# Other costs in the engine model by which a two-tile transformer kernel orders its instructions

## The chip, the cores and the metric

One Trainium2 chip, one core of it. The metric is the device time of one execution in microseconds (us); a run's time is given as the median of several executions. PE is TensorE, DVE is VectorE, ACT is ScalarE, POOL is GpSimd and SP is SyncE, whose queue issues the DMA transfers.

## What is computed

Two blocks of a transformer, one after the other, on x of 256 tokens by 1024 features, in float32, with a memory of 256 tokens. Cut to its outline:

```python
x = first_block(x, mem, ...)      # h = rms_norm(x); p = h @ w_in  (q, k, v, z, xbc, dt, gates)
#   merged = sigmoid(ga) * (stick_breaking_attention(q, k, v) @ w_br_att)
#          + sigmoid(gs) * (ssd_branch(z, xbc, dt) @ w_br_ssm)
#   x += rms_norm(merged @ w_mix_out)
#   x += rms_norm(memory_cross_attention(rms_norm(x), rms_norm(mem)) @ w_xo)
#   x += rms_norm((silu(gate) * up) @ w_down)          # gate, up = rms_norm(x) @ w_gu
x = second_block(x, mem_2, ...)   # two layers: fox (gated causal attention), then mla (latent attention, rope)
#   x += concat(mixer(h), memory_cross(h)) @ w_out
#   u = conv3(rms_norm(x) @ w_up);  x += (silu(u_gate) * u_val) @ w_dn
```

## The kernel before

The 256 tokens are two tiles of 128. A float32 product is made of three products of parts: each value is split into a high part in float32r and a low part, the rest; a product adds high times high, high times low and low times high in PSUM. Weights come by DMA in units of [128, 1024] (512 KB) into one of four raw buffers (`wr`), are copied to a high part (`wh`, normally on ScalarE) and subtracted to a low part (`wl`, on VectorE or GpSimd), and up to ten split units are held. Each unit is used by both tiles and then freed.

The program is written as threads (Python generators): `main(0)` and `main(1)` for the tiles, and others for attention lanes, the state space model, the memory's keys and the preparing of weights. A thread yields what it wants next: an instruction for VectorE, ScalarE or GpSimd (line 263 on), a buffer, a bank of PSUM, or "may TensorE go on" (`start`, lines 351 to 394). `run` (line 396) goes on, over and over, with the thread whose want can start earliest by a model of the engines; small weights for priorities and turns (`BASE`, `TUNE`, lines 56 to 64) are added to that time. What it picks is emitted at once, so this choice fixes the order of instructions in every engine's queue. Each queue then runs in that order on the chip, and waits where an operand isn't ready.

The model (`Model`, line 181) holds one time for each engine, and for every stretch of a buffer the times of its last write and read. `regs` (line 236) puts an instruction at the later of its engine's time and of its operands' times, and adds its cost; `after` (line 210) adds a latency of 0.17 us where another engine wrote the operand, and `SAME` (0.1) where the same one did. The costs are formulas of the number n of elements in a partition, in `Engine` (lines 268 to 292), and numbers given with each product (`mm`, line 538):

```python
if eng == "ACT":   c = 0.00083 * n + 0.08 + 0.09 * small + (0.15 if len(outs) > 1 else 0)
elif eng == "DVE": c = (0.00052 if one and not psum else 0.00104) * n + 0.07 + 0.05 * (small > 0)
else:              c = 0.0021 * n + 0.1          # GpSimd; a power: 0.165 * n + 0.3
```

Some instructions have two forms, of which `start` takes the one that would end first after a bias: a copy on ScalarE or VectorE (`copy`, line 552), the low part of a weight on VectorE or GpSimd (`prepare_low`, line 493: `E.tensor_tensor(L, raw, H, subtract) for E in (V, G)`, GpSimd put back by `POOL`, 0.8 us, or 0.4 in the stage `ssd`).

The whole program is run twice (`model_kernel`, lines 2051 to 2054): a first pass that emits nothing and finds in which order the weight units are wanted, and a second one that emits the instructions and splits the units in that order. The model serves both.

Lines of the profile: 539 is the matmul in `mm`, 543 the transpose in `tr`, 547 a DMA, and 290 the call of any VectorE, ScalarE or GpSimd instruction (the helper in `Engine`).

Of the kernel before, what the change touches and what calls it, by code (L numbers as in the profile page):

```python
# [46 lines left out]
# row table of short vectors  # L47
# [18 lines left out]
NB = 10      # split weight units held  # L66
RAW = 4      # raw weight units held
# [28 lines left out]
class Arena:  # L96
    """Places buffers in one SBUF tile: in the smallest gap, the large ones at its end."""
# [38 lines left out]
class Split:  # L136
    """A value as two float32r parts whose sum is the float32 value."""
# [11 lines left out]
class Joint:  # L149
    """The splits of both tiles' [128 features, 8, 128 tokens]"""  # L150
# [13 lines left out]
class Spare:  # L164
    """A split unit's place that is lent for something else"""
# [15 lines left out]
class Model:  # L181
    """Rough times of the engines, by which the order of instructions is chosen."""

    LAT = 0.17

    def __init__(self):
        self.t = {"PE": 0.0, "DVE": 0.0, "ACT": 0.0, "POOL": 0.0, "DMA": 0.0}
        self.index = {e: i for i, e in enumerate(self.t)}
        self.s = {}
# [14 lines left out]
    def state(self, t):  # L204
        if t not in self.s:
            # times of the last write and the last read, and the engines of these
            self.s[t] = np.zeros((4, ARENA // 8 + 1))
        return self.s[t]

    def after(self, regs, eng, rows):  # L210
        e = 0.0
        for t, lo, hi in regs:
            a = self.state(t)
            for i in rows:
                x = a[2 * i, lo:hi]
                j = x.argmax()
                x = x[j] + ((SAME if eng and not i else 0.0) if a[2 * i + 1, lo + j] == eng else self.LAT)
# [4 lines left out]
    def ready(self, ap, rows=(0,)):  # L222
        """When the tensor engine can use it"""
# [4 lines left out]

    def deps(self, eng, outs, ins):
        i = self.index[eng]  # L230
        # two engines don't read a bank at once
# [17 lines left out]
class Op:  # L249
    """An instruction to be put into its engine's queue in its turn."""  # L250

    def __init__(self, eng, emit, cost, outs, ins, func=None):
        self.eng, self.emit, self.cost, self.func = eng, emit, cost, func
# [4 lines left out]
class Engine:  # L258
    """Makes the instructions of an engine, with their rough costs."""
# [4 lines left out]
    def __getattr__(self, op):  # L264
# [3 lines left out]
        def call(*a, **k):  # L268
# [6 lines left out]
            psum = any(x.tensor.name.startswith("pa") for x in [out] + ins)  # L275
            small = sum(size(x) == 1 for x in ins)
            if eng == "ACT":
# [1856 lines left out]
```

## Time and profile before

| | |
|---|---|
| time of a run, median of 3 | 1334.74 us (1333.91 to 1334.86) |
| span of the profiled execution | 1330.6 us, 22067 instructions; its own time was not recorded apart |
| mean granted TensorE clock | 0.993 of 2.4 GHz |
| matmul busy (PE), weight load busy (PEld) | 97%, 86% of the span |
| VectorE, ScalarE, GpSimd busy | 68%, 61%, 21% |
| HBM | 217.95 MB moved by DMA, 163 GB/s over the span |
| chain that ended last, by engine | PE 79%, DVE 9%, POOL 5%, ACT 3%, issue 2%, DMA 2% |

A matmul's record runs from its issue to its modelled end and overlaps the next one's, so records are longer than the distance from one to the next, and a busy PE can hide short gaps. The span leaves out what lies before the first and after the last instruction, some 4 us here (1334.7 less 1330.6). Idle time of an engine is listed with what ended it.

### The profile page before, as it was taken

The numbers are of one execution on the slowest core, as the hardware profiler recorded it, in microseconds if no ns is written. First come the engines' busy times: TensorE is split into PE (matmuls) and PEld (weight loads), VectorE is DVE, ScalarE is ACT, GpSimd is POOL, SyncE is SP. The second block draws the span as 40 slices with busy tenths as digits, with TensorE's granted clock in tenths as the row PEclk, the third lists the DMA queues.
The fourth block names the chain that finished last, engine by engine and source line by source line (L and its number), as shares of the span: only waits on it lengthen the run. The fifth ranks groups of instructions, "written<-read, shape, count | busy, mean of one in ns | idle before, by whom it ended". The sixth has DMA issues, their size and how long they took to land.

```text
span 1330.6 us, 22067 instructions
## 1 busy us (share of the span) xinstructions
PE 1289.8 (97%) x8376; PEld 1146.3 (86%) x8376; DVE 909.7 (68%) x1471; ACT 816.8 (61%) x1481; POOL 285.1 (21%) x364
## 2 busy tenths in 40 slices
PE   8999999999999999999998899998999989999998
PEld 6989998898888887999997788788999867799997
DVE  6567688877677537655556567898665897786664
ACT  6567677766646547544456566785554785865552
POOL 3052203333022002000014521102111463031110
PEclk9999999999999999999999999998999999999999
DMA  8632543544664624756552343566654333365650
GB/s 270 219 112 96 195 154 107 180 158 143 216 211 159 227 73 143 246 183 188 190 192 96 127 143 112 191 221 221 190 185 144 115 112 99 131 223 189 185 173 32
DMA packets 62457, 217.95 MB, mean 164 GB/s; under 512 B 7440, under 2 KB 7568, under 8 KB 62352
## 3 DMA queue, kind: packets, MB, share of 16 engines
q1 hardware_dynamic: 62352, 216.56, 49.9%
q8 instruction: 65, 1.06, 0.3%
q14 instruction: 40, 0.33, 0.1%
HBM read 215.48 MB, written 1.05 MB: 163 GB/s over the span
## 4 chain that ended last, share of the span: by engine, by line
PE 79%; DVE 9%; POOL 5%; ACT 3%; issue 2%; DMA 2%; SPq 0%; DVEq 0%; POOLq 0%; ACTq 0%
PE pa L539 75%; DVE arena L290 6%; POOL arena L290 4%; PE pa L543 3%; DVE wl L290 2%; ACT arena L290 2%; POOL small L290 1%; ACT wh L290 1%; DVE arena_r L290 1%; DMA wr<-in_w_in 1%; ACT arena_r L290 0%; DMA arena<-in_mem 0%; DMA wr<-in_w_up 0%; DMA wr<-in_w_dn 0%; SPq L547 0%
## 5 line engine op out<-in xcount | busy, mean ns | idle before, releaser
L539 PE MATMUL pa<-wh,arena_r 128*128 128x512 f32 (+2 forms) x1812 | 590.8, 395 | 3.6 <-DVE arena_r L290 1.6
L290 DVE TENSOR_TENSOR wl<-wr,wh 128x1024 fp32r<-128x1024 f32 (+2 forms) x353 | 432.4, 1233 | 219.9 <-ACT wh L290 214.4
L290 ACT ACTIVATE wh<-wr 128x1024 fp32r<-128x1024 f32 (+3 forms) x393 | 406.2, 1044 | 246.5 <-PE pa L539 200.2
L539 PE MATMUL pa<-arena_r,wh 128*128 128x256 f32 (+2 forms) x2736 | 495.5, 283 | 0.0
L539 PEld LDWEIGHTS pa<-arena_r,wh 128*128 128x128 f32 (+2 forms) x2736 | 425.6, 190 | 4.3 <-issue 0.3
L539 PEld LDWEIGHTS pa<-wh,arena_r 128*128 128x128 f32 x1812 | 342.3, 190 | 73.2 <-DVE arena_r L290 3.3
L539 PE MATMUL pa<-arena_r,wl 128*128 128x256 f32 (+2 forms) x1368 | 385.5, 282 | 0.0
L539 PE MATMUL pa<-wl,arena_r 128*128 128x512 f32 (+2 forms) x906 | 353.2, 390 | 4.2 <-DVE wl L290 4.1
L539 PEld LDWEIGHTS pa<-arena_r,wl 128*128 128x128 f32 (+2 forms) x1368 | 259.9, 190 | 0.2
L290 POOL TENSOR_TENSOR wl<-wr,wh 128x1024 fp32r<-128x1024 f32 (+2 forms) x53 | 131.0, 2476 | 568.0 <-ACT wh L290 543.7
L539 PEld LDWEIGHTS pa<-wl,arena_r 128*128 128x128 f32 x906 | 172.0, 190 | 35.4 <-DVE wl L290 5.4
L290 ACT ACTIVATE arena<-pa 128x512 f32<-128x512 f32 (+4 forms) x142 | 78.5, 563 | 73.8 <-PE pa L539 58.9
L290 DVE SCALAR_TENSOR_TENSOR arena<-pa,cols,arena 128x255 f32<-128x255 f32 (+2 forms) x208 | 89.1, 476 | 31.2 <-ACT arena L290 29.6
L290 DVE TENSOR_TENSOR arena<-arena 128x512 f32<-128x512 f32 (+4 forms) x117 | 90.8, 792 | 23.1 <-POOL arena L290 13.3
L290 ACT ACTIVATE arena<-arena 128x512 f32<-128x512 f32 (+5 forms) x126 | 76.6, 615 | 33.7 <-DVE arena L290 30.6
L539 PE MATMUL pa<-arena 128*64 128x128 f32 (+4 forms) x888 | 91.2, 286 | 3.2 <-POOL arena L290 1.7
L539 PEld LDWEIGHTS pa<-arena 128*64 128x64 f32 (+3 forms) x888 | 78.1, 160 | 16.4 <-issue 5.5
L543 PE MATMUL pa<-ident,arena 128*128 128x128 f32 (+3 forms) x494 | 73.1, 278 | 18.1 <-DVE arena L290 14.0
L543 PEld LDWEIGHTS pa<-ident,arena 128*128 128x128 f32 (+3 forms) x494 | 56.8, 138 | 33.9 <-DVE arena L290 19.1
L290 POOL TENSOR_SCALAR small<-small 128x1 f32<-128x1 f32 x38 | 17.4, 459 | 265.6 <-ACT arena L290 186.9
L290 ACT ACTIVATE arena<-pa,cols 128x256 f32<-128x256 f32 x92 | 44.8, 566 | 28.2 <-PE pa L539 28.2
L290 ACT ACTIVATE arena<-pa,small 128x128 f32<-128x128 f32 (+4 forms) x126 | 44.5, 416 | 21.9 <-PE pa L539 21.6
(123 smaller groups left out, 769.8 us busy)
## 6 DMA issues: line engine op xcount, KB each, us to landing
wr<-in_w_up SPq DMA_DIRECT2D x96, 512.0 KB, 4.0
wr<-in_w_in SPq DMA_DIRECT2D x80, 512.0 KB, 4.3
wr<-in_w_gu SPq DMA_DIRECT2D x44, 512.0 KB, 4.1
wr<-in_w_dn SPq DMA_DIRECT2D x44, 512.0 KB, 4.2
wr<-in_w_down SPq DMA_DIRECT2D x22, 512.0 KB, 4.0
wr<-in_w_fox SPq DMA_DIRECT2D x20, 512.0 KB, 3.3
wr<-in_w_br_ssm SPq DMA_DIRECT2D x16, 512.0 KB, 4.2
wr<-in_w_xkv SPq DMA_DIRECT2D x16, 512.0 KB, 4.1
```

The source lines that it names most:

```text
L290: emit = (lambda: f(*a, **k)) if f else (lambda: None)
L539: self.T.matmul(out, l, r, start=start, stop=stop, skip_group_check=True)
L543: self.T.transpose(out, in_, self.const["ident"][:k, :k])
```

## The change

Comments and docstrings are left out of the changed file, which changes no instruction. The rest lies in the model; no thread asks for another instruction, and `BASE`, `TUNE` and the other weights keep their values.

- **Latencies.** Instead of 0.17 us for any other engine: by the writer (`LAT`: PE 0.205, DVE 0.118, ACT 0.136, POOL 0.06) plus by the reader (`USE`: PE 0.02, POOL 0.05, DMA 0.1); for the same engine `OWN` (DVE 0.118, ACT 0.136, POOL 0.03) instead of `SAME`.
- **Products.** `mm` no longer takes a cost; `product` works it out from the shape and type. A product of 256 columns in float32r goes from 0.109 to 0.120 us, of 512 from 0.216 to 0.227, a pair's half in float32 from 0.2 to 0.115.
- **A shared port.** One time, `port`, for the VectorE instructions with two operands in SBUF, or with one and none in PSUM, and for GpSimd's with any input: such an instruction starts no earlier than the last of them ended, in `start` as in `regs`.
- **The matmul clock.** After a wait of TensorE over a limit, its instructions cost 1.9 times as much for 3 us.
- **Costs.** GpSimd's instructions cost more: 0.25 us plus 0.0023 n (a power 0.45 plus 0.165 n), copies and memsets less than that; ScalarE's differ by 0.03 us at most, but for those with an accumulated sum; a DMA lands 0.4 us later.

```diff
-    LAT = 0.17
+    LAT = {"PE": 0.205, "DVE": 0.118, "ACT": 0.136, "POOL": 0.06, "DMA": 0.0}
+    USE = {"PE": 0.02, "DVE": 0.0, "ACT": 0.0, "POOL": 0.05, "DMA": 0.1}
+    OWN = {"PE": 0.0, "DVE": 0.118, "ACT": 0.136, "POOL": 0.03, "DMA": 0.0}
...
-                x = x[j] + ((SAME if eng and not i else 0.0) if a[2 * i + 1, lo + j] == eng else self.LAT)
+                k = int(a[2 * i + 1, lo + j])
+                x = x[j] + ((0.0 if i else self.own[eng]) if k == eng else self.lat[k] + self.use[eng])
...
+    def product(l, r):
+        m, n = Model.region(l)[3], Model.region(r)[3]
+        if l.dtype == F32:
+            return 0.115 if m <= 64 and n == 128 else 2 * max(0.111, n / 1200 + 0.0025)
+        return max(0.06, n / 2400 + (0.0135 if m > 32 else 0.0067))
...
-    def regs(self, eng, cost, outs, ins):
+    def regs(self, eng, cost, outs, ins, port=False):
         i = self.index[eng]
-        e = self.t[eng] = max(self.t[eng], self.deps(eng, outs, ins)) + cost
+        s = max(self.t[eng], self.deps(eng, outs, ins), self.port if port else 0.0)
+        if eng == "PE":
+            if s - self.t[eng] > 2.8:
+                self.cold = s + 3.0
+            if s < self.cold:
+                cost *= 1.9
+        e = self.t[eng] = s + cost
+        if port:
+            self.port = e
         if eng == "DMA":
-            e += 1.5
+            e += 1.9
...
             if eng == "ACT":
-                c = 0.00083 * n + 0.08 + 0.09 * small + (0.15 if len(outs) > 1 else 0)
+                c = 0.00083 * n + (0.07 if psum else 0.11) + 0.08 * small + (0.187 if len(outs) > 1 else 0)
             elif eng == "DVE":
-                one = len([x for x in ins if size(x) > 1]) < 2 and op != "tensor_reduce"
-                c = (0.00052 if one and not psum else 0.00104) * n + 0.07 + 0.05 * (small > 0)
+                one = len(big) < 2 and op != "tensor_reduce"
+                port = sum(not space(x) for x in big) > 1 or one and not psum and n > 32
+                c = (0.00052 if one and not psum else 0.00104) * n + 0.075 + 0.05 * (small > 0)
...
             else:
-                c = 0.0021 * n + 0.1
+                port = bool(ins)
+                c = 0.0023 * n + 0.25
                 if k.get("op") == OP.pow:
-                    c = 0.165 * n + 0.3
-                if op == "affine_select":
-                    c = 0.001 * n + 0.1
+                    c = 0.165 * n + 0.45
+                elif op == "affine_select":
+                    c = 0.00145 * n + 0.1
+                elif op == "tensor_copy":
+                    c = 0.001 * n + 0.19
+                elif op == "memset":
+                    c = 0.0009 * n + 0.07
...
-                s = max(m.t[a.eng], a.dep)
+                s = max(m.t[a.eng], a.dep, m.port if a.port else 0.0)
...
-    def mm(self, out, l, r, start, stop, cost):
+    def mm(self, out, l, r, start, stop):
         self.T.matmul(out, l, r, start=start, stop=stop, skip_group_check=True)
-        self.model.op("PE", cost, [out], [l, r])
+        self.model.op("PE", Model.product(l, r), [out], [l, r])
...
-        self.model.op("DMA", n / 360e3 + 0.05, o, [])
+        self.model.op("DMA", n / 380e3 + 0.05, o, [])
```

In `big` are the inputs with more than one element in a partition, and `space` tells whether an operand lies in PSUM. In all threads the fourth number of `mm` is dropped; `SAME` and `PAIR` go.

## Rows read from the trace of the kernel before

**Rows 1.** Part 1 of the page: busy time of each engine, its share of the span, and the number of its instructions.

```profile
PE 1289.8 (97%) x8376; PEld 1146.3 (86%) x8376; DVE 909.7 (68%) x1471; ACT 816.8 (61%) x1481; POOL 285.1 (21%) x364
```

**Rows 2.** The table of busy times by stretch, over the stages of the program: from and to in us, length, then busy us and instructions of PE (matmul), PEld (weight load), DVE (VectorE), ACT (ScalarE) and POOL (GpSimd), the granted clock as a share of 2.4 GHz, the DMA share and GB/s. The first stretch is the start, 532 to 699 holds the column blocks of `w_gu` for both tiles, 699 to 765 the start of the `fox` layer, 1031 to 1164 most of the `mla` layer, the last one the end.

```profile
0.00:12.00 12.00, 6.42 (x32) 5.35 (x32) 3.81 (x6) 6.32 (x15) 1.65 (x9) 0.99 0.78 269
...
532.24:698.57 166.33, 166.33 (x1152) 155.59 (x1151) 90.11 (x97) 81.71 (x110) 4.22 (x8) 1.00 0.62 200
698.57:765.10 66.53, 59.30 (x307) 48.04 (x305) 42.77 (x84) 39.63 (x90) 32.66 (x69) 0.95 0.34 111
...
898.15:931.42 33.27, 29.86 (x184) 26.84 (x184) 27.18 (x36) 19.31 (x28) 7.28 (x4) 0.90 0.66 221
...
1031.21:1164.28 133.07, 123.39 (x748) 101.92 (x747) 111.67 (x252) 97.70 (x238) 51.31 (x68) 1.00 0.35 114
...
1326.00:1330.60 4.60, 0.69 (x4) 0.23 (x2) 1.37 (x2) 0.00 (x0) 0.00 (x0) 0.87 0.37 139
```

**Rows 3.** The groups of TensorE's instructions with their shapes kept apart, of the stretch from 598.77 to 632.03 us alone: busy us, mean ns of one, and idle time before.

```profile
L539 PE MATMUL pa<-arena_r,wh 128*128 128x256 f32 x125 | 22.7, 283 | 0.0
L539 PE MATMUL pa<-arena_r,wl 128*128 128x256 f32 x63 | 17.8, 283 | 0.0
L539 PE MATMUL pa<-wh,arena_r 128*128 128x512 f32 x32 | 10.2, 390 | 0.0
L539 PE MATMUL pa<-wl,arena_r 128*128 128x512 f32 x16 | 6.2, 391 | 0.0
```

**Rows 4.** The table of busy times by stretch, of that same stretch and of three others that hold the longest waits of TensorE.

```profile
598.77:632.03 33.26, 33.26 (x236) 31.34 (x235) 16.75 (x18) 15.14 (x18) 0.00 (x0) 1.00 0.60 188
904.00:918.00 14.00, 10.59 (x38) 8.24 (x38) 12.04 (x20) 7.46 (x10) 0.35 (x1) 0.76 0.53 177
720.00:730.00 10.00, 7.53 (x49) 6.24 (x49) 5.04 (x12) 4.98 (x11) 4.41 (x16) 0.83 0.19 59
740.00:752.00 12.00, 8.90 (x38) 7.03 (x37) 3.16 (x8) 3.07 (x7) 6.88 (x16) 0.86 0.28 89
```

**Rows 5.** Who waited for whom, TensorE's matmuls alone: engine and line, what it waited for, us in total, times, the longest.

```profile
PE pa L543 <- DVE arena L290: 14.0, 10, 2.6
PE pa L539 <- POOL arena L290: 4.1, 3, 2.5
PE pa L539 <- DVE wl L290: 4.1, 2, 3.4
PE pa L539 <- POOL small L290: 3.1, 1, 3.1
```

**Rows 6.** VectorE's groups with their shapes kept apart, over the whole span. `wl<-wr,wh` is the low part of a weight unit; a `pa` on the right is an operand in PSUM.

```profile
L290 DVE TENSOR_TENSOR wl<-wr,wh 128x1024 fp32r<-128x1024 f32 x340 | 422.0, 1249 | 214.1 <-ACT wh L290 208.6
L290 DVE TENSOR_TENSOR arena<-arena 128x512 f32<-128x512 f32 x79 | 71.1, 920 | 14.3 <-ACT arena L290 7.1 <-POOL arena L290 6.0
...
L290 DVE SCALAR_TENSOR_TENSOR arena_r<-pa,cols,arena_r 128x128 fp32r<-128x128 f32 x150 | 41.9, 342 | 2.3 <-ACT arena_r L290 2.2
L290 DVE SCALAR_TENSOR_TENSOR arena<-arena,cols 128x128 f32<-128x128 f32 x80 | 36.5, 473 | 6.2 <-ACT arena L290 5.4
...
L290 DVE TENSOR_TENSOR arena<-pa,arena 128x512 f32<-128x512 f32 x37 | 25.3, 687 | 12.5 <-PE pa L539 11.4 <-ACT arena L290 1.1
```

**Rows 7.** The low parts on VectorE from 532.24 to 665.30 us, a stretch without work on GpSimd.

```profile
L290 DVE TENSOR_TENSOR wl<-wr,wh 128x1024 fp32r<-128x1024 f32 x51 | 62.5, 1225 | 50.9 <-ACT wh L290 49.6
```

**Rows 8.** GpSimd's groups with their shapes kept apart, over the whole span; `mhalf` marks the power of -1/2, and the one with 12 elements is of the `softplus` polynomial.

```profile
L290 POOL TENSOR_TENSOR wl<-wr,wh 128x1024 fp32r<-128x1024 f32 x50 | 127.2, 2549 | 398.9 <-ACT wh L290 374.6 <-DMA wr<-in_w_up 14.5 <-DVE wl L290 9.8
L290 POOL TENSOR_TENSOR small<-small,mhalf 128x1 f32<-128x1 f32 x36 | 24.3, 675 | 2.9
...
L290 POOL TENSOR_SCALAR arena<-arena 128x12 f32<-128x12 f32 x18 | 7.4, 410 | 9.6 <-ACT arena L290 8.2
...
L290 POOL TENSOR_TENSOR arena<-arena 128x12 f32<-128x12 f32 x18 | 5.7, 318 | 2.9 <-DVE arena L290 1.6
```

**Rows 9.** The instructions in order of time around 897 to 911 us: start, us, engine, line, operation, and in brackets the idle time before with what ended it.

```profile
896.72 4.81 POOL L290 TENSOR_TENSOR wl<-wr,wh 128x1024 fp32r<-128x1024 f32 x2 [9.76 <-DVE wl L290]
...
897.06 2.21 DVE L290 SCALAR_TENSOR_TENSOR arena<-arena,cols 128x128 f32<-128x128 f32 x1 [0.37 <-ACT arena L290]
...
899.20 2.62 DVE L290 TENSOR_TENSOR arena_r<-arena,arena_r 128x256 fp32r<-128x256 f32 x1
...
901.74 3.14 DVE L290 SCALAR_TENSOR_TENSOR arena<-arena,cols 128x128 f32<-128x128 f32 x3
...
901.82 2.53 POOL L290 TENSOR_TENSOR wl<-wr,wh 128x1024 fp32r<-128x1024 f32 x1 [0.28 <-ACT wh L290]
...
910.98 0.79 PE L539 MATMUL pa<-wl,arena_r 128*128 128x512 f32 x1 [3.41 <-DVE wl L290]
```

**Rows 10.** The same view at the two triangular products of the `fox` layer's gates (`fox_gate`), one for each tile.

```profile
723.81 0.39 PE L539 MATMUL pa<-small,triu 128*128 128x12 f32 x2 [2.47 <-POOL arena L290]
...
745.45 0.40 PE L539 MATMUL pa<-small,triu 128*128 128x12 f32 x2 [3.10 <-POOL small L290]
```

**Rows 11.** The same view at the zeroing of a key buffer near the start.

```profile
18.14 2.12 DVE L290 TENSOR_SCALAR arena<-arena,small 128x512 f32<-128x512 f32 x1 [0.46 <-POOL small L290]
18.17 3.84 POOL L290 MEMSET arena<- 64x2048 f32 x2
```

More of the change, by code (lines that the diff above doesn't have):

```diff
@@ L188, in __init__ @@
         self.index = {e: i for i, e in enumerate(self.t)}
+        self.lat = [self.LAT[e] for e in self.t]
+        self.use = [self.USE[e] for e in self.t]
+        self.own = [self.OWN[e] for e in self.t]
+        self.port = self.cold = 0.0
         self.s = {}
@@ L249, with __init__ @@
 class Op:
-    def __init__(self, eng, emit, cost, outs, ins, func=None):
-        self.eng, self.emit, self.cost, self.func = eng, emit, cost, func
+    def __init__(self, eng, emit, cost, outs, ins, func=None, port=False):
+        self.eng, self.emit, self.cost, self.func, self.port = eng, emit, cost, func, port
         self.outs, self.ins = ([Model.region(x)[:3] for x in y] for y in (outs, ins))
@@ L274, in call @@
             n = size(a[1] if op == "tensor_reduce" else out)
-            psum = any(x.tensor.name.startswith("pa") for x in [out] + ins)
+            space = lambda x: x.tensor.name.startswith("pa")
+            psum = any(space(x) for x in [out] + ins)
             small = sum(size(x) == 1 for x in ins)
+            big = [x for x in ins if size(x) > 1]
+            port = False
             if eng == "ACT":
-                c = 0.00083 * n + 0.08 + 0.09 * small + (0.15 if len(outs) > 1 else 0)
+                c = 0.00083 * n + (0.07 if psum else 0.11) + 0.08 * small + (0.187 if len(outs) > 1 else 0)
             elif eng == "DVE":
-                one = len([x for x in ins if size(x) > 1]) < 2 and op != "tensor_reduce"
-                c = (0.00052 if one and not psum else 0.00104) * n + 0.07 + 0.05 * (small > 0)
+                one = len(big) < 2 and op != "tensor_reduce"
+                port = sum(not space(x) for x in big) > 1 or one and not psum and n > 32
+                c = (0.00052 if one and not psum else 0.00104) * n + 0.075 + 0.05 * (small > 0)
                 if op == "reciprocal":
@@ L284, in call @@
             else:
-                c = 0.0021 * n + 0.1
+                port = bool(ins)
+                c = 0.0023 * n + 0.25
                 if k.get("op") == OP.pow:
-                    c = 0.165 * n + 0.3
-                if op == "affine_select":
-                    c = 0.001 * n + 0.1
+                    c = 0.165 * n + 0.45
[5 more added lines that the diff above has]
+                    c = 0.0009 * n + 0.07
             emit = (lambda: f(*a, **k)) if f else (lambda: None)
-            return Op(eng, emit, c, outs, [x for x in ins if x.tensor.name[:3] != "in_"])
+            return Op(eng, emit, c, outs, [x for x in ins if x.tensor.name[:3] != "in_"], port=port)
         return call
@@ L442, in issue @@
                     self.real.preload_act_table_set(s)
-                self.model.t["ACT"] += 1.3
+                self.model.t["ACT"] += 1.29
                 self.table = s
         a.emit()
-        self.model.regs(a.eng, a.cost, a.outs, a.ins)
+        self.model.regs(a.eng, a.cost, a.outs, a.ins, a.port)
     def begin_unit(self, key):
@@ L620, in proj @@
                 xh, xl = X.H[:, k0 + k, :], X.L[:, k0 + k, :]
-                self.mm(out, xh, H[:, kk, :], k == 0, False, c)
-                self.mm(out, xh, L[:, kk, :], False, False, c)
-                self.mm(out, xl, H[:, kk, :], False, k == nk - 1, c)
+                self.mm(out, xh, H[:, kk, :], k == 0, False)
+                self.mm(out, xh, L[:, kk, :], False, False)
+                self.mm(out, xl, H[:, kk, :], False, k == nk - 1)
         return b
@@ L681, in proj_thin @@
         for k in range(8):
-            self.mm(out, H[:, k, :], X.H[:, k, :], k == 0, False, 0.056)
-            self.mm(out, L[:, k, :], X.H[:, k, :], False, False, 0.056)
-            self.mm(out, H[:, k, :], X.L[:, k, :], False, k == 7, 0.056)
+            self.mm(out, H[:, k, :], X.H[:, k, :], k == 0, False)
+            self.mm(out, L[:, k, :], X.H[:, k, :], False, False)
+            self.mm(out, H[:, k, :], X.L[:, k, :], False, k == 7)
         return b
@@ L1092, in dt_both @@
             xh, xl = (x[:, k] for x in X.both)
-            self.mm(out, H[:, k, :], xh, k == 0, False, 0.109)
-            self.mm(out, L[:, k, :], xh, False, False, 0.109)
-            self.mm(out, H[:, k, :], xl, False, k == 7, 0.109)
+            self.mm(out, H[:, k, :], xh, k == 0, False)
+            self.mm(out, L[:, k, :], xh, False, False)
+            self.mm(out, H[:, k, :], xl, False, k == 7)
         w = yield ("b", 256)
@@ L1277, in ssd_quad @@
                     self.mm(y, st["xdt", n, g].ap[:, 64 * e8:64 * e8 + 64], ev[:, 4 * v + i + j, :],
[L1278 removed]
+                            n == 0, n == t)
         E.free()
@@ L1305, in ssd_out @@
         b = self.bank()
-        self.mm(b[1][:, 0:1], sqs.ap, const["ones"][:, 0:1], True, True, 0.42)
+        self.mm(b[1][:, 0:1], sqs.ap, const["ones"][:, 0:1], True, True)
         sqs.free()
@@ L1740, in fox_gate @@
         p = self.bank()
-        self.mm(p[1][:, :12], const["triu"], sp, True, t == 0, 0.42)
+        self.mm(p[1][:, :12], const["triu"], sp, True, t == 0)
         if t:
-            self.mm(p[1][:, :12], const["ones"], st["fsp", 0], False, True, 0.42)
+            self.mm(p[1][:, :12], const["ones"], st["fsp", 0], False, True)
         yield self.act(cum.ap, p[1][:, :12], "Copy")
```

53 lines of the change are left out of this document (25 added, 28 removed).

## The prediction

> **What bounds the kernel now.** I read the page's busy times first. The matmul rows cover 1289.8 of 1330.6 us, so 40.8 us are left in which TensorE does nothing, against 421 us on VectorE and 514 on ScalarE [rows 1]. The table by stage comes next, and shows two kinds of stage. From 532 to 699 us, with the column blocks for both tiles, TensorE is busy for 166.33 of 166.33 us; no order of the other queues can shorten that. In the `fox` stage it is idle for 7.2 of 66.5 us, around 898 to 931 for 3.4 of 33.3, in the `mla` stage for 9.7 of 133 [rows 2]. The start up to 12 us has 5.6 us of idle time, and after 1326 us there are 3.9 us of last additions and output [rows 2]: both hang on first loads and last stores, and I count them as fixed. So 40.8 - 5.6 - 3.9 = 31.3 us of idle time lie in the middle. To that comes the clock: right after three of the waits the granted clock over 14, 10 and 12 us is 0.76, 0.83 and 0.86 of full speed [rows 4], part of each stretch at 1.2 instead of 2.4 GHz. Such a stretch loses 14 x 0.24 + 10 x 0.17 + 12 x 0.14 = 3.4 + 1.7 + 1.7 = 6.8 us. **In reach of an order are about 31.3 + 6.8 = 38 us.**
>
> Who ends TensorE's waits is the last view: VectorE's arena work 14.0 us in ten waits, GpSimd 4.1 and 3.1, VectorE's low parts of weights 4.1 [rows 5]. Every single one is 3.4 us or less, and none of the four largest entries is a transfer. That is a queue-order problem, not a lack of an engine.
>
> That matmul busy understates what is left is the rule in the Trainium skill's page Perfetto Trace Analysis, section Identifying the Most-Contended Engine, which wants weight-load busy time instead. By it the sum would have more room: in the full stretch weight loads take 155.59 of 166.33 us, 93.5% [rows 2], and 1146.3 / 0.935 is 1226 us [rows 1], 105 us under the span. I take 38 us, from the idle rows, since the load of a transpose or of a small product is shorter and would count as room that no order can use.
>
> **Part by part.** No instruction is added or taken away, except where an instruction has two forms; so each edit acts through the order alone, and its price is what waits it makes or ends.
>
> *Products.* In a full stretch 188 products of 256 columns and 48 of 512 [rows 3] fill 33.26 us [rows 4]. The old costs give 188 x 0.109 + 48 x 0.216 = 30.9 us, 7% too fast; the new ones 188 x 0.120 + 48 x 0.227 = 33.5 us. So the old plan believes that TensorE runs ahead of VectorE and ScalarE more than it does, and the new one is right to 1%. By itself this moves no wait in a full stretch, as TensorE covers everything there. In the thin stages it pulls the model's readiness nearer to the truth. I count it as zero: the cover is a TensorE queue that is never empty. If that cover is gone, the price is a wait like those listed, about 1 us each.
>
> *GpSimd's costs.* A small step of the `softplus` polynomial cost 0.125 us in the model and takes 0.32 to 0.41 on the chip, a power of one column 0.465 against 0.675, a low part 2.25 against 2.55 [rows 8]; the new formulas give 0.28, 0.615 and 2.6. The chain behind a gate has 19 such steps. The old plan takes it to be done about 19 x 0.24 = 4.5 us too early, and puts the triangular product into TensorE's queue then; in the chip's order everything behind it on TensorE waits with it. That is the 2.47 and 3.10 us at 724 and 745 us [rows 10], with 1.7 us of clock each: 9.0 us in all. With the truer cost other products go first if they are there; these are the tile's column blocks, which both tiles share out. I take half, **-4.5 us**, between nothing (no product was left) and all 9.
>
> *The port.* The trace shows that VectorE and GpSimd hold each other up. Low parts on VectorE take 1.225 us where GpSimd rests [rows 7] and 1.249 on the mean; the two-operand work in SBUF of 512 elements 0.920 on the mean, when the same with an operand in PSUM takes 0.687; 128-column multiply-adds 0.473 against 0.342 [rows 6]. Held time: 340 x 0.024 + 79 x 0.233 + 80 x 0.131 = 8.2 + 18.4 + 10.5 = 37 us of VectorE, from 50 low parts on GpSimd of 2.55 us and some smaller work [rows 8]. The old model knows nothing of it and hands GpSimd a low part whenever VectorE's queue looks long. The worst case stands at 897 us: three low parts, 4.81 + 2.53 us, under which three steps of VectorE take 2.21, 2.62 and 3.14 us [rows 9]. The first and the third are one and three multiply-adds of 0.34 us, the second lies with 256 elements between 0.34 and 0.69, say 0.45 [rows 6]; so they lose 1.9 + 2.2 + 2.1 = 6.2 us. Then TensorE waits 3.41 us for a low part on VectorE [rows 9] and loses 3.4 us of clock: 6.8 us. The new model makes the second taker wait for the first, so it sees this coming. **-5 us**, between 0 and 6.8.
>
> *What the port costs.* A low part now goes to GpSimd only where VectorE stands still on PSUM work. If all 50 moved, VectorE would have 50 x 1.225 = 61 us more and 37 less: 934 us, 70% of the span. That is no bound on the mean; in the `mla` stage, where VectorE has 111.7 of 133 us [rows 2], it can be one for some microseconds. GpSimd's small steps are also put later, behind VectorE's two-operand work.
>
> *Zeroing.* The change leaves GpSimd's memsets out of the port (no input). Near the start a one-operand VectorE step takes 2.12 us under a memset [rows 11]. So the model is blind there for two memsets of 1.9 us; TensorE has other work, so I add nothing, up to +2 us. The Trainium skill's page SBUF — State Buffer, section SBUF: two separate sides, has the exclusive pair of ports, and exempts GpSimd work that reads nothing only against VectorE work with two SBUF inputs; that row agrees, and by this rule the change's exemption is too wide.
>
> *Latencies, the clock rule, DMA, ScalarE.* Hops become 0.03 us shorter to 0.055 us longer and ScalarE's costs move by as little; no row prices a hop alone. They break ties, with either sign; bounds from the waits' own size, -3 to +3 us together, zero taken. The clock rule makes work after a long wait look slow, which doesn't remove the wait.
>
> *The rest.* Of the 31.3 us, 3.4 + 2.5 + 3.1 = 9.0 are in the two sites above. The other 22.3 us are short waits, the largest group the ten of 1.4 us on the mean in which a transpose stood in TensorE's queue before VectorE had its operand [rows 5]. A wait ends only where other work was there to go first; I take a third: **-7.4 us**.
>
> *New waits.* The weights `WT`, `POOL`, `HIGH`, `COPY` were set for the old model, and a changed first pass reorders the weight units too; every stage is shuffled. A reshuffle makes waits of the kind that it ends: I take eight of 1 us, **+8 us**, between +2 and +25.
>
> Sum: -4.5 - 5 - 7.4 + 8 = -8.9 us. Against the profiled 1330.6 us of span this is 1321.7; the 4.1 us around it stay, so from the median of 1334.7 it is **1326 us**.
>
> **The rivals.** *VectorE's queue (slower).* The low parts that leave GpSimd stand on VectorE in front of what TensorE awaits. Each costs 1.225 us there. The gross gain of 16.9 us is used up when 14 of the 50 moved parts lie ahead of an awaited result; with 21 of them it is 1334.7 - 16.9 + 21 x 1.225 = 1343.5, plus or minus what the new waits are. For: VectorE is already 84% busy in `mla`, 82% around 898 [rows 2]. Against: a moved part also frees the 0.7 us or so that it held VectorE (37 / 50), and 514 idle ScalarE us can take copies. *Nothing (same).* New waits of 17 us eat the gross gain, as within their bounds of +2 to +25 they can, or the new costs leave most choices as they are, so that the change does not do what it says: 1334.7, within 1332 to 1337. For: where TensorE is full there is nothing to win, and in the thin stages a wait may only move to the next result. *Deep gain.* The waits at the two sites go wholly (-15.8), half of the rest too (-11), and few new ones come (+5): 1313. For: the old model's errors are large, 7% on products and threefold on GpSimd's small steps. Against: a greedy choice by earliest start looks no step ahead, so a better clock doesn't start a chain earlier.
>
> **Numbers.** Forecast case (1319 to 1332) 0.45, deep gain (1306 to 1319) 0.15, same 0.14, slower (1337 to 1350) 0.26. A measurement of this kernel tells 0.2%, 2.7 us, from no change: faster 0.60, same 0.14, slower 0.26. The range leaves out half of the deep gain below 1312 and a good part of the slower case above 1342; for gains alone it is 1313 to 1331.
>
> **What would show it.** Right: no half-clock stretch after 900 us; matmul waits on GpSimd near zero; far fewer than 50 low parts on GpSimd; the 512-element step near 0.69 us; PE idle near 32 us. Wrong: TensorE's waits on `wl` grow, VectorE over 95% in `mla`, or new half-clock stretches; and if the low parts on GpSimd stay about 50, the port doesn't act as I read it.

## The result and the profile after

The changed kernel takes **1345.79 us** (median of 4, 1344.70 to 1347.40) against 1334.77 for the kernel before on the same chip: ratio 1.0091, interval 1.0075 to 1.0107. It is slower by 0.9%; the forecast was 1326 us, and the time lies above the range. The profiled execution took 1344.9 us, 2.1 more than its span of 1342.8. The two spans differ by 12.2 us, the medians by 11.0: the 4.1 us that the forecast put around the span of before came from two different executions.

Part 1 of the page, as [rows 1]:

```profile
PE 1297.2 (97%) x8376; PEld 1152.1 (86%) x8376; DVE 911.3 (68%) x1502; ACT 822.1 (61%) x1485; POOL 204.8 (15%) x331
```

The same 8376 products; GpSimd has 80 us less to do, VectorE as much as before, and TensorE is idle for 45.6 us where it was 40.8. The stages of [rows 2]:

```profile
0.00:12.00 12.00, 7.56 (x33) 6.30 (x34) 4.17 (x7) 6.30 (x15) 1.64 (x9) 0.95 0.81 277
532.24:698.57 166.33, 166.33 (x1143) 155.33 (x1143) 88.42 (x93) 81.06 (x108) 1.32 (x4) 1.00 0.60 200
698.57:765.10 66.53, 60.87 (x313) 50.19 (x312) 39.74 (x85) 42.75 (x95) 28.92 (x67) 0.92 0.31 103
898.15:931.42 33.27, 33.27 (x236) 31.33 (x236) 27.99 (x44) 22.12 (x32) 0.00 (x0) 1.00 0.66 228
1031.21:1164.28 133.07, 115.47 (x689) 94.70 (x688) 103.54 (x242) 91.08 (x227) 33.26 (x61) 0.96 0.30 99
```

The stretch at 898 us is full now, as forecast. The last one has lost 7.9 us of busy PE and got a clock of 0.96 where it was 1.00. Two shorter stretches by the same view, the second without a like before the change:

```profile
720.00:732.00 12.00, 6.77 (x35) 5.47 (x34) 4.19 (x12) 5.04 (x15) 4.98 (x20) 0.68 0.04 14
1064.00:1074.00 10.00, 4.01 (x24) 3.26 (x19) 5.98 (x13) 4.24 (x7) 7.11 (x6) 0.75 0.02 8
```

TensorE's waits, as [rows 5]:

```profile
PE pa L579 <- DVE arena L326: 10.1, 8, 5.2
PE pa L579 <- ACT arena L326: 7.9, 3, 4.3
PE pa L575 <- ACT arena L326: 6.5, 11, 1.1
PE pa L575 <- POOL arena L326: 4.5, 1, 4.5
...
PE pa L575 <- DVE wl L326: 2.2, 4, 0.8
```

Waits on low parts have halved (4.1 to 2.2). But single waits are longer: 5.2, 4.5 and 4.3 us, where none was over 3.4. And 14.4 us now end with ScalarE's arena work, for which the same view of the kernel before has 3.4:

```profile
PE pa L543 <- ACT arena L290: 2.3, 2, 1.7
...
PE pa L539 <- ACT arena L290: 1.1, 3, 0.6
```

VectorE's forms, as [rows 6], and GpSimd's low parts, as [rows 8]:

```profile
L326 DVE TENSOR_TENSOR wl<-wr,wh 128x1024 fp32r<-128x1024 f32 x370 | 452.4, 1238 | 201.5 <-ACT wh L326 196.5
L326 DVE TENSOR_TENSOR arena<-arena 128x512 f32<-128x512 f32 x79 | 59.6, 772 | 12.1 <-ACT arena L326 9.4 <-POOL arena L326 0.5
L326 DVE SCALAR_TENSOR_TENSOR arena<-arena,cols 128x128 f32<-128x128 f32 x80 | 27.0, 349 | 3.9 <-ACT arena L326 2.9
...
L326 DVE TENSOR_TENSOR arena<-pa,arena 128x512 f32<-128x512 f32 x37 | 25.1, 688 | 12.1 <-PE pa L575 10.7 <-ACT arena L326 1.4
```

```profile
L326 POOL TENSOR_TENSOR wl<-wr,wh 128x1024 fp32r<-128x1024 f32 x20 | 51.6, 2581 | 134.2 <-ACT wh L326 131.4 <-DVE arena L326 1.4 <-issue 1.3
```

So the port was read rightly, as far as VectorE goes: 30 low parts left GpSimd, the 512-element step in SBUF went from 0.920 to 0.772 us, the multiply-add of 128 columns from 0.473 to 0.349, and the form with an operand in PSUM stayed at 0.688. That is 79 x 0.148 + 80 x 0.124 = 21.6 us of VectorE back, for 30 x 1.238 = 37 us of new low parts. None of it shows on TensorE, whose idle time grew.

**Where the 12.2 us came from.** I cut the span at the first and last products for both tiles (256 columns, with `wh` or `wl` on the right) of the three large column blocks. The three blocks themselves take 150.2, 136 and 150.4 us when full; between them lie the stages in which an order matters. Two kernels with the same products can be compared stage by stage in this way, even though their instructions stand in another order:

| us | to `w_gu` | `w_gu` | to `w_up` 0 (`fox`) | `w_up` 0 | to `w_up` 1 (`mla`) | `w_up` 1 | tail | span |
|---|---|---|---|---|---|---|---|---|
| before | 539.4 | 150.2 | 197.3 | 142.4 | 135.6 | 150.5 | 15.2 | 1330.6 |
| after | 541.6 | 150.2 | 200.2 | 136.2 | 148.8 | 150.4 | 15.4 | 1342.8 |

The gain of 6.2 us at the port's worst site is there (`w_up` 0), and `mla` alone gives back 13.2. That stage in the table of busy times, of before and then of after:

```profile
1029.30:1164.90 135.60, 125.92 (x760) 104.06 (x759) 113.48 (x254) 100.23 (x242) 51.93 (x68) 1.00 0.36 116
```

```profile
1028.20:1177.00 148.80, 131.20 (x761) 107.68 (x759) 114.06 (x261) 101.77 (x244) 33.26 (x61) 0.97 0.32 104
```

Idle PE grew from 9.7 to 17.6 us, +7.9; the same 760 products were busy for 5.3 us more at a mean clock of 0.97. Together they are the 13.2 us. The part at the lower clock is the less certain one: e4, further down, has the stage in the very order of before and took 136.7 us at a mean clock of 0.98.

```profile
1024.40:1161.10 136.70, 128.74 (x761) 106.51 (x760) 112.52 (x254) 100.21 (x242) 50.47 (x68) 0.98 0.35 115
```

VectorE is busy 114.06 of 148.8 us, 77%, less than the 84% of before, so on the mean it doesn't bound the stage.

**What such a wait looks like.** The longest wait after the change, in order of time (ScalarE's and weight-load rows left out). A head norm squares on ScalarE, adds up on VectorE (to 128x8), takes a power on GpSimd (`mhalf`) and multiplies on VectorE:

```profile
1066.47 0.29 POOL L326 TENSOR_SCALAR arena<-arena 128x8 f32<-128x8 f32 x1 [2.95 <-DVE arena L326]
...
1066.84 1.67 POOL L326 TENSOR_TENSOR arena<-arena,mhalf 128x8 f32<-128x8 f32 x1
1067.35 0.95 DVE L326 TENSOR_REDUCE arena<-arena 128x8 f32<-128x768 f32 x1 [0.70 <-ACT arena L326]
...
1068.55 0.96 DVE L326 TENSOR_TENSOR arena<-arena 128x768 f32<-128x768 f32 x1 [0.24 <-POOL arena L326]
1068.60 1.01 POOL L326 TENSOR_SCALAR arena<-arena 128x8 f32<-128x8 f32 x1
1069.42 0.94 DVE L326 TENSOR_REDUCE arena<-arena 128x8 f32<-128x768 f32 x1
...
1069.56 1.94 PE L579 MATMUL pa<-ident,arena 128*96 128x128 f32 x8 [5.22 <-DVE arena L326]
1069.69 1.67 POOL L326 TENSOR_TENSOR arena<-arena,mhalf 128x8 f32<-128x8 f32 x1
```

Head norms of three chunks go through the three engines one behind the other, and TensorE has nothing but their transposes. A head norm of the kernel before:

```profile
1097.91 3.23 POOL L290 TENSOR_TENSOR arena<-arena,mhalf 128x8 f32<-128x8 f32 x1
...
1099.51 1.75 PE L539 MATMUL pa<-arena 128*64 128x128 f32 x16
...
1101.11 2.38 POOL L290 TENSOR_TENSOR wl<-wr,wh 128x1024 fp32r<-128x1024 f32 x1
1101.12 0.47 PE L539 MATMUL pa<-wh,arena_r 128*128 128x512 f32 x1
...
1101.17 3.14 DVE L290 TENSOR_TENSOR arena<-arena 128x768 f32<-128x768 f32 x1 [0.86 <-POOL arena L290]
...
1101.67 0.63 PE L539 MATMUL pa<-wh,arena_r 128*128 128x512 f32 x2
...
1104.37 0.64 PE L543 MATMUL pa<-ident,arena 128*96 128x128 f32 x4 [1.61 <-DVE arena L290]
```

There the two steps are far slower, 3.23 and 3.14 us, the multiplication held up by a low part on GpSimd, just what the new model avoids. But TensorE meanwhile has another group's values and products with split weights, and waits 1.61 us. In this pair the slow chain with cover cost less than the fast chain without.

### The profile page after: what moved, and what is told of

It reads as the page before. It is cut to its first block, busy times and chain, and to the rows that moved or that the text cites. A ratio compares the mean times of both kernels' runs of the same rounds, so it can differ in the third digit from the quotient of the medians.

```text
span 1342.8 us, 22025 instructions
## 1 busy us (share of the span) xinstructions
PE 1297.2 (97%) x8376; PEld 1152.1 (86%) x8376; DVE 911.3 (68%) x1502; ACT 822.1 (61%) x1485; POOL 204.8 (15%) x331
## 4 chain that ended last, share of the span: by engine, by line
PE 86%; DVE 5%; ACT 4%; POOL 2%; issue 1%; DMA 1%; SPq 0%; ACTq 0%; POOLq 0%; DVEq 0%
PE pa L575 83%; PE pa L579 3%; DVE arena L326 3%; ACT arena L326 2%; POOL arena L326 1%; ACT wh L326 1%; DVE wl L326 1%; POOL small L326 1%; ACT arena_r L326 1%; DVE arena_r L326 0%; DMA wr<-in_w_in 0%; DMA wr<-in_w_up 0%; ACT L478 0%; SPq L583 0%; DVE wh L326 0%
## 5 line engine op out<-in xcount | busy, mean ns | idle before, releaser
L326 DVE TENSOR_TENSOR wl<-wr,wh 128x1024 fp32r<-128x1024 f32 (+2 forms) x386 | 464.6, 1219 | 207.8 <-ACT wh L326 200.8
L326 ACT ACTIVATE wh<-wr 128x1024 fp32r<-128x1024 f32 (+4 forms) x393 | 407.8, 1044 | 280.9 <-PE pa L575 214.0
L326 ACT ACTIVATE arena<-pa 128x512 f32<-128x512 f32 (+4 forms) x132 | 73.3, 565 | 71.2 <-PE pa L575 57.7
L575 PE MATMUL pa<-arena 128*64 128x128 f32 (+4 forms) x888 | 94.4, 290 | 6.8 <-ACT arena L326 6.1
L326 POOL TENSOR_SCALAR small<-small 128x1 f32<-128x1 f32 x38 | 21.0, 552 | 492.4 <-ACT arena L326 437.3
L579 PE MATMUL pa<-ident,arena 128*128 128x128 f32 (+3 forms) x494 | 74.7, 284 | 18.1 <-DVE arena L326 10.1
L326 DVE TENSOR_TENSOR arena<-arena 128x512 f32<-128x512 f32 (+4 forms) x117 | 75.0, 657 | 17.7 <-ACT arena L326 10.5
L326 POOL TENSOR_TENSOR wl<-wr,wh 128x1024 fp32r<-128x1024 f32 x20 | 51.6, 2581 | 134.2 <-ACT wh L326 131.4
L326 ACT ACTIVATE arena<-pa,small 128x128 f32<-128x128 f32 (+6 forms) x125 | 42.8, 419 | 27.9 <-PE pa L575 27.6
```

The lines of the kernel that those rows point to most:

```text
L326: emit = (lambda: f(*a, **k)) if f else (lambda: None)
L575: self.T.matmul(out, l, r, start=start, stop=stop, skip_group_check=True)
L579: self.T.transpose(out, in_, self.const["ident"][:k, :k])
```

## The experiments

The old and the new model stood in one file, each edit behind a switch, so that a kernel can take the new costs in part, from a stage on, or in one of the two passes. The edits below are shortened to what they amount to. All results, with the stages as above (us; the full blocks and the tail, alike within 0.8 us but for e14's tail of 19.5, are left out):

| kernel | time | ratio to before, interval | to `w_gu` | `fox` | `w_up` 0 | `mla` |
|---|---|---|---|---|---|---|
| after | 1345.79 | 1.0091 (1.0075 to 1.0107) | 541.6 | 200.2 | 136.2 | 148.8 |
| e1 new, no port | 1342.46 | 1.0066 (1.0047 to 1.0086) | 542.4 | 207.6 | 136.2 | 138.9 |
| e2 old, port alone | 1348.55 | 1.0127 (1.0060 to 1.0195) | 547.0 | 205.4 | 136.1 | 144.9 |
| e3 first pass old, second new | 1345.38 | 1.0103 (1.0035 to 1.0172) | 535.9 | 202.3 | 136.2 | 155.7 |
| e4 first pass new, second old | **1328.03** | 0.9953 (0.9940 to 0.9967) | 538.6 | 199.5 | 136.1 | 136.7 |
| e5 new, old from `mla` on | 1331.56 | 0.9981 (0.9970 to 0.9992) | 542.2 | 200.5 | 136.1 | 135.5 |
| e6 new, rope in its own thread | 1341.33 | 1.0052 (1.0016 to 1.0089) | 541.4 | 200.3 | 136.1 | 145.9 |
| e7 old, latency 0.18 | 1346.16 | 1.0097 (1.0060 to 1.0134) | 547.1 | 203.7 | 136.2 | 142.2 |
| e8 old, `WT` 0.33 | 1344.56 | 1.0080 (1.0045 to 1.0114) | 538.5 | 199.1 | 142.6 | 147.3 |
| e9 old, low parts of `mla` on VectorE | 1332.27 | 0.9986 (0.9972 to 1.0001) | 539.7 | 199.2 | 142.2 | 134.5 |
| e10 new, low parts of `mla` to GpSimd | 1352.66 | 1.0146 (1.0123 to 1.0169) | 541.8 | 200.7 | 136.1 | 154.7 |
| e11 new, no port from `mla` on | 1339.60 | 1.0047 (1.0030 to 1.0063) | 540.3 | 200.0 | 136.2 | 145.1 |
| e12 combination | 1333.41 | 0.9995 (0.9984 to 1.0006) | 536.0 | 205.1 | 136.1 | 135.1 |
| e13 new, tile 1 ahead in `mla` | 1337.62 | 1.0039 (1.0023 to 1.0055) | 539.4 | 199.9 | 136.2 | 144.3 |
| e14 old, tile 1 behind in `mla` | 1355.79 | 1.0190 (1.0160 to 1.0220) | 538.8 | 199.4 | 141.6 | 153.5 |
| e15 e4 with tile 1 ahead in `mla` | 1341.45 | 1.0069 (1.0051 to 1.0087) | 538.7 | 199.3 | 136.2 | 150.2 |
| e16 as e13, half as much | 1340.28 | 1.0064 (1.0042 to 1.0087) | 540.4 | 197.7 | 136.2 | 146.1 |

**Which edit, which pass?** e1 takes the port out of the changed kernel, e2 puts it alone into the one before; e3 and e4 give each pass its own model.

```diff
-            return Op(eng, emit, c, outs, [x for x in ins if x.tensor.name[:3] != "in_"], port=port)   # e1
+            return Op(eng, emit, c, outs, [x for x in ins if x.tensor.name[:3] != "in_"], port=False)
-        self.model = Model(NEW)                       # e3; e4 has OLD and NEW the other way round
+        self.model = Model(OLD if plan else NEW)
```

Expected of e1:

> The changed kernel with the shared port left out of the model, all other new costs kept. Port theory (the serialised port takes low parts from GpSimd and delays the short chains of the mla stage): the mla stage, 13 us longer after the change, falls back by most of it, total 1332 to 1337. Reshuffle theory (any other costs make another order, whose waits fall by chance, and no single edit carries the loss): anywhere from 1330 to 1350, and the mla stage need not be what moves. Unit-order theory (the first pass wants the weight units in another order): 1346, as the first pass keeps nearly all new costs.

Of e2:

> The kernel before with the shared port alone put into the model. Port theory: the loss comes with it, 1343 to 1350. Reshuffle theory: anywhere from 1330 to 1350. Unit-order theory: near 1335 unless the port changes the first pass.

Of e3:

> The changed kernel, but the first pass, which fixes the order of the weight units, uses the old model; the second pass, which fixes the queues, the new one. Unit-order theory: 1333 to 1337. Port theory: the second pass carries the port, so 1343 to 1349. Reshuffle theory: anywhere from 1330 to 1350.

Of e4:

> The reverse: the first pass with the new model, the second with the old one. Unit-order theory: 1344 to 1348. Port theory: 1333 to 1337. Reshuffle theory: anywhere from 1330 to 1350.

Without the port 1342.46 us, with it alone 1348.55: the loss comes with the port alone and with all the other edits without it, so the port isn't what carries it; the other edits weren't taken apart. In e1 `mla` did fall, to 138.9 us, as the port theory wants, but `fox` rose to 207.6; e11 below puts the question to `mla` again. The order of units isn't it either: with the old one (e3) the loss stays, and with the new one and old costs behind it (e4) the kernel is *faster* than both, 1328.03 us. All four have the gain in `w_up` 0, e4 too, where GpSimd has as many low parts as before (53 of all shapes). In e4 even the clash of [rows 9] is still there, with the same three low parts on GpSimd and VectorE steps as long as before, and TensorE is full all the same:

```profile
897.88 4.91 POOL L335 TENSOR_TENSOR wl<-wr,wh 128x1024 fp32r<-128x1024 f32 x2 [9.49 <-ACT wh L335]
898.22 2.32 DVE L335 SCALAR_TENSOR_TENSOR arena<-arena,cols 128x128 f32<-128x128 f32 x1
900.46 2.62 DVE L335 TENSOR_TENSOR arena_r<-arena,arena_r 128x256 fp32r<-128x256 f32 x1
902.98 2.39 POOL L335 TENSOR_TENSOR wl<-wr,wh 128x1024 fp32r<-128x1024 f32 x1 [0.18 <-PE pa L586]
903.00 3.17 DVE L335 SCALAR_TENSOR_TENSOR arena<-arena,cols 128x128 f32<-128x128 f32 x3
```

```profile
898.00:912.00 14.00, 14.00 (x83) 12.44 (x83) 13.62 (x18) 8.73 (x16) 7.19 (x3) 1.00 0.65 179
```

So there the gain in `w_up` 0 doesn't come from keeping the two engines apart.

**Is it the costs in `mla`, and there one late block?** In the changed kernel tile 1's second product with `w_mla` comes 50.7 us into the stage, behind the rotation of the latent key (`rope`), before the change at 31.0. e5 takes the old costs from `mla` on, in both passes; e6 keeps the new ones and lets the rotation run beside the product; e7 and e8 are edits of the old model that mean nothing.

```diff
     def stage(self, name):
+        if name == "mla": self.model.set_costs(OLD)   # e5
-        yield from self.rope(t, kr[:, None, :], 1)      # e6, waited for before kr is used
+        erope = self.spawn(self.rope(t, kr[:, None, :], 1), 0, self.cur.turn)
-    LAT = 0.17                                          # e7
+    LAT = 0.18
-BASE = dict(WT=0.3, ...                                # e8
+BASE = dict(WT=0.33, ...
```

Expected of e5:

> The changed kernel, whose model goes back to the old costs from the stage mla on (in both passes), so that all up to there is ordered by the new one. Starved-block theory (in the mla stage the new model puts tile 1's second w_mla product and what hangs on it late, behind tile 0's short steps): the mla stage is 135 to 138 us instead of 148.8, the stages before stay as after the change, total 1330 to 1335. Reshuffle theory: the mla stage 138 to 150.

Of e6:

> The changed kernel, where the six rope steps of the latent key run in a thread of their own, so that tile 1's second w_mla product does not stand behind them. In the order of the queue the product then has 27.5 us of TensorE's work before it in the stage, as against 35.6 after the change and 28.5 before it. Starved-block theory: mla stage 135 to 141 us, total 1331 to 1338. Reshuffle theory: the stage changes by chance, 140 to 152. Port theory in the sense of VectorE's load (GpSimd has no low part left in the stage): still 145 to 150.

Of e7:

> The kernel before with the old model and its one latency at 0.18 instead of 0.17 us: a change that means nothing, to see what a reshuffle costs. Reshuffle theory (the old order was a lucky one among many): the fox and mla stages together 5 to 20 us longer, total 1340 to 1352. Starved-block theory: tile 1's product keeps its place (28.5 us of work before it), so the mla stage 135 to 139, total 1332 to 1339.

Of e8:

> The same with the old model and the weight of turns at 0.33 instead of 0.30, a second meaningless change. Reshuffle theory: 1340 to 1352. Starved-block theory: mla stage 135 to 139, total 1332 to 1339.

e5 shows that the loss of `mla` is made within it: 135.5 us, behind stages ordered by the new costs. In e6 the block came at 30.3 us and the stage was 145.9, only 2.9 us shorter, where the theory wanted 135 to 141; it fell. e7 and e8 are the result I had not looked for in the prediction: 0.01 us of latency costs 12.4 us (1346.16 against 1333.78), a tenth more weight of the turns 10.8, as much as the whole change. e8 loses nearly all of it in `mla` (147.3), e7 in three stages: 7.7 us up to `w_gu`, 6.4 in `fox`, 6.6 in `mla`.

**VectorE's queue.** The rival of the prediction that has the right sign: low parts that left GpSimd delay what TensorE awaits. In `mla` GpSimd had 7 low parts before and none after. e9 moves them in the old model, e10 moves some back in the new one, e11 takes the port out from `mla` on, in both passes; e12 puts together what did well.

```diff
+        'mla': dict(POOL=9.0),                         # e9, old model; also in 'norm_ffn_2.1'
-        'mla2': dict(SWITCH=0.5)}
+        'mla2': dict(SWITCH=0.5, POOL=9.0)}            # e10: -1.0, new model, 'mla' and 'mla2' alone
+        if name == "mla": self.model.port_off()        # e11
+        plan pass: OLD, NEW from "ffn" on; second pass: NEW, OLD from "fox" on   # e12
```

Expected of e9:

> Old model and old order up to the second attention layer (mla); from there on the low weight parts are put on VectorE (the second form's bias 0.8 -> 9.0), so that the seven that GpSimd made in that stage before go to VectorE, as they do after the change. VectorE's-queue theory: these parts stand in front of what TensorE awaits, the stage grows from 135.6 to about 146 to 149 us and the time to about 1345. Refit theory (the settings were chosen with the old costs, any edit of the rules in this stage draws another order, whatever it says of the port): one more draw, between 136 and 149 us, with no tie to the parts. A stage of 138 us or less takes the queue theory away.

Of e10:

> New model as in the changed kernel, and in mla the low parts are drawn to GpSimd (bias 0.8 -> -1.0; five more of them go there). VectorE's-queue theory: the stage falls from 148.8 to about 139 to 141 us and the time to about 1337. Refit theory: the stage stays among 142 to 152 us and the time near 1340 to 1349.

Of e11:

> New model throughout, but from mla on without the shared port; everything ahead of the stage is the changed kernel's. If the port is what costs in this stage: about 139 us as in the variant without the port anywhere (138.9), time about 1336. If the entry state or the other new costs weigh as much: 143 to 150 us, time 1340 to 1347.

Of e12:

> Put together from the stages that each model did best: first pass with the old costs up to ffn and the new ones behind it, second pass with the new costs up to fox and the old ones behind it. If the stages add up: 536 to the first joint product of w_gu, then 150, 199, 136, 136, 150.5 and 15, a span of about 1323 and a time of about 1325 us, below the 1328.0 of new-then-old passes. If orders don't add up (each stage depends on the state in which it is entered): 1328 to 1340.

Both tests go against it. e9's stage, then e10's:

```profile
1031.30:1165.80 134.50, 126.94 (x760) 106.00 (x759) 110.43 (x258) 100.41 (x244) 39.00 (x63) 0.97 0.35 117
```

```profile
1028.80:1183.50 154.70, 132.71 (x761) 108.35 (x760) 113.22 (x258) 100.56 (x241) 40.22 (x66) 0.94 0.31 101
```

With five of the seven low parts gone from GpSimd the old order is no slower (134.5 us); with five back there the new one is *longer* (154.7, 22 us of idle PE). VectorE's busy time differs by 2.8 us between them. The refit theory, that any edit draws a stage of a common size, did no better on these two: e9 lies below its 136 to 149 us, e10 above its 142 to 152. e11 gives back 3.7 of the 13 us, so the port explains little of this stage either. e12's parts don't add up: its start (536.0) and `mla` (135.1) are as hoped, `fox` became 205.1 in place of 199.

**The order of the two tiles.** Tile 1's three chunks (four heads each) begin with their products with `w_q_up`: in the changed kernel 72.0, 78.2 and 84.9 us into the stage, before at 46.2, 55.2 and 83.8, so spread. e13, e16 and e15 put tile 1 ahead, e14 puts it behind.

```diff
     def mla(self, t, x, l):
+        if t: self.cur.turn = X        # and the spawned latent and chunk threads of tile 1
# e13: X = -1 (new model); e16: -0.5 (new); e14: +1 (old); e15: -0.2 (e4's models)
```

Expected of e13:

> New model as in the changed kernel; in mla alone tile 1's thread and its children are preferred (turn 0.2 or 0 -> -1, by 0.3 us of start time). Late-tile theory: in the changed kernel tile 0's work is taken first wherever it can start, tile 1's three chunks then come bunched and TensorE has nothing beside their head norms; with tile 1 ahead the stage falls from 148.8 to 136 to 140 us, the empty PE time in it from 17.6 to about 10, and the time to about 1335. Refit theory: one more draw of the new costs, 145 to 156 us, time 1341 to 1353.

Of e14:

> Old model as in the kernel before; in mla alone tile 1 is put back (turn -> +1, by 0.3 us), which brings its first head transposes as late in the stage's products as the change does (after 64 us of products; 62 in the changed kernel, 53 before). Late-tile theory: the stage grows from 135.6 to 146 to 150 us, the time to about 1345, though no price of the old model is touched. If the new prices themselves misplace single instructions: the stage stays near 136 us, the time near 1334.

Of e15:

> The best version so far (new costs in the first pass, old in the second, 1328.0) with tile 1 preferred by 0.06 us in mla. Late-tile theory: tile 1's last chunk comes ten us of products earlier (66 where it was 78), the stage falls from 136.7 to 130 to 135, the time to 1322 to 1327. If tile 1's chain is not what sets the stage: 136 to 145 us, time 1328 to 1336.

Of e16:

> As the new model with tile 1 ahead, but by half as much (turn -0.5). The first of tile 1's w_mla products comes as early (after 25 us of products), its five later head transposes are bunched (after 65 to 67 us). Late-tile theory, if it is the bunch of chunks that costs: 142 to 147 us, time 1338 to 1344; if it is the start of tile 1's first block: 136 to 140 us, time about 1335. Refit theory: 145 to 156 us.

e14 has what the late-tile theory wants, without any new cost: chunks at 68.4, 73.6 and 78.8 us, a stage of 153.5:

```profile
1030.00:1183.50 153.50, 132.02 (x761) 107.19 (x760) 113.68 (x251) 105.70 (x248) 45.22 (x66) 0.97 0.32 103
```

So holding tile 1 back makes a loss of this size without any new cost, and more of it than the 146 to 150 us expected. The other way the theory holds in part at best: tile 1 ahead gave 144.3 and 146.1 in place of 148.8, where 136 to 140 was expected of e13; and in e15 it made the good order bad (136.7 to 150.2, outside both expectations), with tile 0's third group of scores at 75.6 us where it was 59.6. Nor is a late, bunched tile 1 needed for a long stage: e6 has its chunks at 51.9, 58.7 and 71.3 us. That the stage is short only in a narrow balance of both tiles would fit these runs; it isn't shown. Early tile 1 is no rule.

**What remains.** Put the orders of `mla` beside each other. In e4 and e12, whose second pass orders `mla` by the old costs, every instruction of TensorE, VectorE, ScalarE and GpSimd in the stage stands as in the kernel before, by the names and shapes in the traces; in e5 all but a handful do. These four took 135.6 (before), 136.7, 135.1 and 135.5 us, though what came ahead of the stage was another in each. So it is the order within the stage that sets its time, and the four are one order, drawn once. Where a rule or cost in the stage is another there are fourteen further kernels: e9, with low parts alone moved, is as short (134.5), and thirteen lie between 138.9 and 155.7, mean 147.5 us. Not all thirteen are independent: e3 and e10 come near the order of the changed kernel. Its 148.8 us is about the mean of these. The old order is thus a good one, most edits leave it, and the change does. That the old settings were fitted to this stage isn't shown. Which of the many choices within the stage makes the difference isn't settled either, nor whether settings chosen anew for the new costs would come below 135.

## Why the prediction was wrong

- **The failed step is "New waits".** I took +8 us, eight waits of 1 us over the whole program, beside gross gains of 16.9. Measured: +13.2 in `mla` (+7.9 idle, +5.3 of busy time at a lower clock), +2.9 in `fox`, +2.2 up to `w_gu`: 18.3 us. It is the net growth of these stages. It lies within the bounds of +2 to +25, but I put it near the lower one by the step "a reshuffle makes waits of the kind that it ends". It doesn't: the longest new ones are 4.3 to 5.2 us, and the granted clock is low around them, 0.75 over ten us around 1064, 0.68 over twelve around 720. And I counted old waits as faults of the model, when the old order was itself a good draw: e7 and e8 left it and cost 11 to 12 us without any reason in the costs.
- **Latencies, zero between -3 and +3: the bounds were too narrow.** They came from the size of the waits. e7 moves one latency by 0.01 us and nothing else, and costs 12.4 us: a small edit too is priced by the order that comes out of it, not by its own size.
- **The port, -5: right at its site, for another reason.** The waits at 897 to 911 us and their low clock are gone, -6.2 us in that stage. But five kernels whose second pass ordered this stage without the port lose them too (e1, e4, e7, e12 and e15), so another order was enough; and in e4 TensorE doesn't wait although VectorE is held up as before. That the clash made the wait of 3.41 us was read from their nearness in time. What was right is VectorE's share: 21.6 us came back there.
- **GpSimd's costs, -4.5: not there.** The two triangular products waited 2.47 and 3.10 us [rows 10]; now the first waits 4.46, the second 0.43:

```profile
724.73 0.60 PE L575 MATMUL pa<-small,triu 128*128 128x12 f32 x2 [4.46 <-POOL arena L326]
...
751.87 0.28 PE L575 MATMUL pa<-small,triu 128*128 128x12 f32 x1 [0.43 <-POOL small L326]
```

  The second wait is all but gone and the first has grown: 5.57 us together then, 4.89 now, at the granted clock of 0.68 around the first. That is about the lower bound of nothing that I had named. Whether another product was left to go ahead of the first one isn't shown.
- **The rest, -7.4: not there.** Idle PE grew by 4.8 us in all. A third of the short waits was a number without a row behind it.
- **The rivals.** The slower case's time, 1343.5, was near by luck: its mechanism was wrong, since e9 and e10 both contradict it, `wl` waits fell to 2.2 us, and VectorE has 77% in `mla`. With e7 and e8 known, a chance of 0.26 for a slower kernel was too low. Of the signs named as right, three came (no half clock at 900, 20 low parts on GpSimd, the 512-element step nearer to 0.69) with the time still longer, and two did not: TensorE still waits 4.5 us for GpSimd at one place, and is idle for 45.6 us instead of 32. The three watched the engines that the edit is about, not the one that bounds. "New half-clock stretches" was the sign named as wrong that came.
- **Where the argument against a deep gain stood, the forecast's weak point stood too**: a greedy choice by earliest start looks no step ahead. Truer costs therefore start no chain earlier by themselves; they change which of nearly equal starts goes first.

## What to carry to other kernels

Where a planner takes the earliest start by a model, its order is one draw, and an edit of its costs, however true, is first of all a new draw: measure some edits that mean nothing before forecasting one that means something, and take their spread into the range. Two gave +11 and +12 us here; all sixteen edited kernels lie between 5 us below and 22 above the kernel before. Compare stage by stage between products that both kernels have in common, and judge a faster side engine by whether TensorE has other work at that moment. With the order open, draw several and keep the best: e4, 0.5% below the kernel before, keeps the old order of `mla` and has the gain in `w_up` 0; it came out of such a draw, not out of the better model.

## What the runs showed of the hardware

- A two-operand step of VectorE in SBUF stood still for nearly the whole of GpSimd's instruction: the 768-element multiplication took 3.14 us when begun 0.06 us behind a low part of 2.38, and 0.96 without. GpSimd's side is held as well: an addition on 128x8 took 1.01 us beside that step and 0.29 without. The Trainium skill's page SBUF — State Buffer, section SBUF: two separate sides, calls the port pair an exclusive lock, not a bandwidth split; these rows agree with it.
- A side engine that is held up less was worth nothing by itself here: there are 21.6 us less of it on VectorE, and while the waits of transposes on VectorE's arena work went from 14.0 to 10.1 us, those of transposes and other products on ScalarE's rose by 11.0 (3.4 to 14.4).
